# Output projection behind an RWKV scan: PSUM tiles, load queues, load order, and the engine of two group norms

## Chip, cores and metric

The kernel runs on one core of a Trainium2 chip. The metric is the device time of one execution in microseconds (us). TensorE is called PE (its weight loads PEld), VectorE DVE, ScalarE ACT, GpSimd POOL and SyncE SP, as in the profile. ACTq and SPq are DMA issues on the queues of ACT and SP.

## What is computed

One step of a two-layer diffusion trunk with model width 1024 over 640 tokens: 512 latent tokens and 128 prompt tokens. Layer 0 mixes tokens with a bidirectional RWKV-7 scan, layer 1 with neighbourhood attention, and each is followed by a squared-ReLU MLP. The change lies at the end of layer 0's mixer, which in the reference is this, with `ys` the outputs of the forward and the backward scan:

```python
y = (ys[0] + ys[1]).astype(jnp.float32)
mean = jnp.mean(y, axis=-1, keepdims=True)
var = jnp.mean(jnp.square(y - mean), axis=-1, keepdims=True)
yn = ((y - mean) * lax.rsqrt(var + GN_EPS)).reshape(B, T, D) * ln_w + ln_b
o = (yn + (bonuses[0] + bonuses[1]).reshape(B, T, D)) * g
return o.astype(h.dtype) @ w_o, jnp.stack(finals, axis=1)
...
x = x + gt1[:, None, :] * o
```

## The kernel before

**Layout and arithmetic.** The activations lie with the 1024 features on 8 blocks of 128 partitions and the 640 tokens along the free axis. A product of two f32 matrices is made from three fp32r products: each operand is split into a high part (a cast on ACT) and a low part (a subtraction), and PE adds high x high, high x low and low x high in PSUM. So a weights block of 1024 x 128 goes through a DMA of 512 KB, a cast on ACT and a subtraction on DVE before PE can use it.

**The scan and the group norms.** `phase_scan` runs the recurrence in five steps of four sub-steps, two directions at a time. PSUM is fully shared out here: two banks `A0`, `A1` for the products of the directions, two banks `B0`, `B1` for their running state (`self.G`), and two tiles `pp0`, `pp1` of two banks each. When both directions have passed a half of a 128-token tile, `post_half` (L1114) takes that half: it loads V, the bonus factors `bc` and the gates `gs` (SP, L1129 to L1131), subtracts the mean (L1139), squares (ACT, L1140), makes the inverse root in many small DVE steps (`rsqrt`, L252), does five more operations on 128 x 512 elements (L1146, L1147, L1149 to L1151), turns the result with four PE transposes into `pp1` (L1154), multiplies by the gates (DVE, L1160) and stores it to a DRAM scratch, `o_d` (SP, L1162). The argument `on_dve` says whether L1139 and the five are put on DVE or on POOL. The last two halves are (3,1), tile 3, and (0,0), tile 0: L844 gives (3,1) to POOL and (0,0) to DVE. The buffer `pbuf`, into which V and the gates are loaded, exists once for each of the two parities of half.

**The first part of the projection.** `wo_first` (L1182) multiplies by `w_o` those 384 tokens whose `o` is finished before the last halves: it runs beside the end of the scan. It goes over 8 output blocks, k0 to k7, each with 24 matmuls of 384 columns (L1219). `weights(k)` loads a block into one of the two `adaraw` buffers on SP (L1189), casts it (L1191) and subtracts (L1192) into one of two `ww` pairs. The products of k go into one half of the two-bank tile `pp0`. The residual input is loaded into one of three `wr` buffers by two DMAs on ACT's queue (L1215, L1216), 128 and 64 KB; DVE multiplies the product by the gate and adds it (L1221, two instructions), and SP stores the sum to a DRAM scratch `xa_d` (L1222). The load into a `wr` buffer has to wait for the store of k-3.

```python
if k % 2 == 0:
    pa = self.pp_tile(0)
ps = pa[:, 512 * (k % 2):512 * (k % 2) + NA]
hi, lo = W[k] if k < 2 else weights(k)
```

**The second part.** `phase_wo` (L1224) does the same for the other 256 tokens, whose `o` came from the last halves. Its buffers lie where the scan's lay. SP loads the residual input `xi` (two DMAs of 512 KB, L1237), then `ol`, the finished `o` (eight of 128 KB, L1242), then the first part's results `xa` (eight, L1251). Each of eight blocks k has 24 matmuls of 256 columns (L1265) into one of four `psl` banks; DVE adds the residual (L1269), which reads `xi`; ACT squares the new x for the next norm (L1271), and PE sums the squares over the features (L359). The MLP of layer 0 follows.

**What sets the order.** The kernel is written as one program, and the order of the instructions on each engine and queue is fixed when it is built (L1587, with a simulated timeline as its guide): an instruction may be taken ahead of an earlier one of its engine if it seems ready. On the chip each engine and queue then keeps that order. The scan's matmuls and, late in the scan, the transposes of `post_half` are chained to one another by hand (`mm`, L850); the matmuls of `wo_first` are not.

Of the kernel before, what the change touches and what calls it, by code (L numbers as in the profile page):

```python
# [8 lines left out]
F32 = mybir.dt.float32  # L9
# [7 lines left out]
P = 128  # L17
D = 1024
KT = 8
TS = 512  # L20
# [152 lines left out]
class K:  # L173
# [248 lines left out]
    def pool(self, st, name, bufs, **k):  # L422
        return st.enter_context(self.tc.tile_pool(name=name, bufs=bufs, reuse_waits="tile", **k))
# [349 lines left out]
    def phase_scan(self, st):  # L773
        nc, tc = self.nc, self.tc
        if True:
            pool = lambda name, bufs, **k: self.pool(st, name, bufs, **k)
            self.yp = pool("yp", 4)
            adp = pool("adp", 2)
            one = pool("one", 1)
            self.ch = pool("ch", 1, space=PSUM)  # L780
            self.post = pool("post", 2)
            self.G = [self.ch.tile([P, 512], F32, name=f"B{d}").rearrange("p (a b v) -> p a b v", a=2, b=4) for d in range(2)]
            self.lnwb = one.tile([P, 2, 256], F32, name="lnwb")
            nc.scalar.dma_start(self.lnwb, self.A["lnwb"].rearrange("p (a x) -> p a x", a=2))
            self.cst2 = st.enter_context(ExitStack())
            self.c_slots(self.pool(self.cst2, "c2", 1), 4, 1)
            for d in range(2):
                self.gu[d].append(one.tile([P, 2, 2, 4, 64], F32, name=f"GU{d}1"))
                for h in range(2):
                    nc.gpsimd.memset(self.gu[d][1][64 - 64 * h:96 - 64 * h, h], 0.0)  # L790
            self.gi = [0, 0]
            self.yt = {}
            self.ydone = {}
            todo, running = [], []
            ada = [(0, b) for b in range(8, 24)]

            def ada_next():
                if ada:
                    pa = self.pp_tile()
                    pa = pa[:, :256]  # L800
                    self.ada_sums.append(self.ada_first(*ada.pop(0), adp, pa, self.mm))

            self.ada_sums = []
            done = {(0, 3): [(4, 0), (4, 1)], (3, 1): [(2, 0), (1, 1)], (3, 3): [(2, 1), (1, 0)],
                    (4, 1): [(3, 0), (0, 1)], (4, 3): [(3, 1), (0, 0)]}
            pend = None
            self.pin = True
            for n, ts in enumerate(self.steps):
                for e in range(4):
                    s0, s1 = (self.chain_step(ts, n, e, d) for d in range(2))  # L810
                    next(s0)
                    if pend:
                        for x in pend:
                            next(x)
                        if n == 4 and not self.late:
                            self.late_pools()
                        for t in done.get((n, e - 1) if e else (n - 1, 3), []):
                            todo.append(self.post_half(*t, n == 4 and t[0] % 3))
                    f = (0, 1, 1, 2)
                    k = self.fill(f[0])  # L820
                    next(s0)
                    k += self.fill(f[1])
                    ada_next()
                    k += self.fill(f[2])
                    next(s1)
                    next(s0)
                    next(s0)
                    next(s1)
                    k = self.fill(f[3])
                    if k:  # L830
                        next(s1)
                    pend = [s1] if k else [s1, s1]
                    for x in running:
                        next(x)
                    m = 2 if n == 4 else 1
                    running, todo = todo[:m], todo[m:]
                    for _ in range(2):
                        for x in running:
                            next(x)
            for x in pend:  # L840
                next(x)
            for x in running:
                next(x)
            todo += [self.post_half(*t, i) for i, t in enumerate(done[4, 3])]  # L844
            for _ in range(3):
                for x in todo:
                    next(x)
            self.wo_first(adp)
# [333 lines left out]
    def wo_first(self, adp):  # L1182

        nc = self.nc
        NA = 384

        def weights(k):
            raw = adp.tile([P, 4, 256], F32, name="adaraw").rearrange("p a x -> p (a x)")
            nc.sync.dma_start(raw, self.A["w_o"][k].rearrange("p a x -> p (a x)"))  # L1189
            hi, lo = (self.wf[1].tile([P, D], F32R, name=f"ww{k % 2}{i}") for i in range(2))  # L1190
            nc.scalar.copy(hi, raw)  # L1191
            nc.vector.tensor_tensor(lo, raw, hi.bitcast(F32), op=ALU.subtract)  # L1192
            return hi, lo

        W = [weights(k) for k in range(2)]
        xs = []
        for f in range(8):
            if f % 2 == 0:
                ol = adp.tile([P, 4, 256], F32, name="adaraw").rearrange("p a x -> p (a x)")
            o = ol[:, NA * (f % 2):NA * (f % 2) + NA]  # L1200
            nc.sync.dma_start(o[:, :256], self.o_d[f, :, 128:384])
            nc.sync.dma_start(o[:, 256:], self.o_d[f, :, TS:])
            hi, lo = (self.wf[0].tile([P, NA], F32R, name=f"wx{f}{i}") for i in range(2))
            nc.scalar.copy(hi, o)
            nc.gpsimd.tensor_tensor(lo, o, hi.bitcast(F32), op=ALU.subtract)
            xs.append((hi, lo))
        gate = self.gate(0, 0)
        xv = self.A["xT"].rearrange("(k p) t -> p k t", p=P)
        for k in range(8):
            if k % 2 == 0:  # L1210
                pa = self.pp_tile(0)
            ps = pa[:, 512 * (k % 2):512 * (k % 2) + NA]
            hi, lo = W[k] if k < 2 else weights(k)
            xi = self.wf[min(k % 3, 1)].tile([P, NA], F32, name=f"wr{k % 3}")
            nc.scalar.dma_start(xi[:, :256], xv[:, k, 128:384])  # L1215
            nc.scalar.dma_start(xi[:, 256:], xv[:, k, TS:])  # L1216
            for f in range(8):
                for j, (a, b) in enumerate(((hi, xs[f][0]), (hi, xs[f][1]), (lo, xs[f][0]))):
                    nc.tensor.matmul(ps, lhsT=a[:, f * P:(f + 1) * P], rhs=b, start=(f == 0 and j == 0), stop=(f == 7 and j == 2))  # L1219
            for a, b, j in ((0, 256, 0), (256, NA, 1)):  # L1220
                nc.vector.scalar_tensor_tensor(xi[:, a:b], ps[:, a:b], gate[:, k, j:j + 1], xi[:, a:b], op0=ALU.mult, op1=ALU.add)  # L1221
            nc.sync.dma_start(self.xa_d[k], xi)  # L1222

    def phase_wo(self):  # L1224

        nc, tc = self.nc, self.tc
        with ExitStack() as st:
# [4 lines left out]
            xp = pool("xp", 8)  # L1232
            sp = pool("sp", 1)
            xv = self.A["xT"].rearrange("(k p) t -> p k t", p=P)
            xi = sp.tile([P, KT, 256], F32, name="xi")
            for o, t in ((0, 0), (P, 384)):
                nc.sync.dma_start(xi[:, :, o:o + P], xv[:, :, t:t + P])  # L1237
            ol = sp.tile([P, KT, 256], F32, name="ol")
            xs = []
            for f in range(0, 8, 2):  # L1240
                for o, t in ((0, 0), (P, 384)):
                    nc.sync.dma_start(ol[:, f:f + 2, o:o + P], self.o_d[f:f + 2, :, t:t + P].rearrange("f p t -> p f t"))  # L1242
            for f in range(8):
                xh = xp.tile([P, 256], F32R, name="xh")
                nc.scalar.copy(xh, ol[:, f])
                xl = xp.tile([P, 256], F32R, name="xl")
                nc.vector.tensor_tensor(xl, ol[:, f], xh.bitcast(F32), op=ALU.subtract)
                xs.append((xh, xl))
# [11 lines left out]
            for k in range(8):  # L1260
                w = self.wblock(self.A["w_o"][k])
                ps = self.psl.tile([P, 512], F32, name="psl")[:, :256]
# [4 lines left out]
                for i, r in enumerate((0, 1, 6, 7)):  # L1267
                    v = lambda a: a[:, 64 * i:64 * i + 64].rearrange("p (g j) -> p g j", g=8)
# [329 lines left out]
```

## Time and profile before

| | |
|---|---|
| median of 3 runs | 2234.46 us (2233.24 to 2239.57) |
| profiled execution, its own time | 2239.71 us |
| span from first to last instruction in it | 2237.9 us |
| mean granted TensorE clock in it | 0.944 |
| PE / DVE / ACT / POOL busy | 90% / 52% / 38% / 20% of the span |
| first part, k0 to k7 (L1219) | 765.3 to 832.7 us |
| second part (L1265) | 841.7 to 872.5 us |

All places are microseconds from the start of the span. "Busy" is the time in which an engine executes an instruction; waits for other engines are told apart from it, and each has a releaser: the instruction that ended last before the waiting one could start. The chain of waits follows these back from the last instruction. An engine that is idle costs nothing unless that chain goes through it. The granted clock is a share of the full 2.4 GHz; 0.5 is 1.2 GHz.

### The profile page before, as it was taken

How to read it: one execution, taken by the hardware profiler on the slowest of the kernel's cores; microseconds unless marked ns; L12 is line 12 of the kernel's file. 1: busy time of each engine (PE TensorE's matmuls, PEld its weight loads, DVE VectorE, ACT ScalarE, POOL GpSimd, SP SyncE). 2: the span in 40 equal slices, each digit the busy share in tenths (PEclk: the TensorE clock that was granted, in tenths of full speed). 3: DMA queues.
4: the chain of work that ended last, by engine and by line, in shares of the span. 5: the costliest groups of instructions: out<-in, count | busy, mean ns of one | idle time of the engine just before them, and what ended most of it. 6: DMA issues, size and time to landing. Idle time of an engine off the chain costs nothing.

```text
span 2237.9 us, 44938 instructions
## 1 busy us (share of the span) xinstructions
PE 2011.6 (90%) x18604; PEld 1827.3 (82%) x18604; DVE 1169.5 (52%) x2592; ACT 857.0 (38%) x1712; POOL 455.1 (20%) x553
## 2 busy tenths in 40 slices
PE   6999988757665569999999999999999999999999
PEld 3777777646554568999999998889677999999999
DVE  6656658387679755433333434433666633434342
ACT  4544553546553414313131323221576331313130
POOL 0001275656542411101010110000232110101010
PEclk8997999978787788999999999999899999999999
DMA  6455764545433464323232223343310232222221
GB/s 242 147 157 155 229 205 135 173 133 166 129 132 96 112 187 141 105 76 111 72 111 76 86 76 119 132 135 92 110 57 31 75 122 76 76 76 76 76 74 69
DMA packets 161037, 260.03 MB, mean 116 GB/s; under 512 B 46528, under 2 KB 102976, under 8 KB 160832
## 3 DMA queue, kind: packets, MB, share of 16 engines
q1 hardware_dynamic: 152224, 244.05, 35.2%
q10 hardware_dynamic: 8608, 13.11, 1.7%
q8 instruction: 146, 2.39, 0.4%
q14 instruction: 59, 0.48, 0.1%
HBM read 218.18 MB, written 37.35 MB: 114 GB/s over the span
## 4 chain that ended last, share of the span: by engine, by line
PE 74%; DVE 13%; DMA 5%; POOL 3%; issue 2%; ACT 2%; SPq 1%; DVEq 0%; ACTq 0%; POOLq 0%
PE psl L205 54%; PE psl L239 3%; DVE invX L996 2%; PE ps L1525 2%; DVE invT L993 2%; POOL C L947 2%; PE po L1562 2%; PE pp L852 2%; PE pt L1550 2%; DVE C L977 1%; PE pp L1219 1%; PE psl L1265 1%; PE psl L286 1%; DMA ld_s<-scr 1%; PE A L852 1%
## 5 line engine op out<-in xcount | busy, mean ns | idle before, releaser
L191 ACT CAST whi<-wraw 128x1024 fp32r<-128x1024 f32 x178 | 186.6, 1049 | 731.5 <-PE psl L205 701.9
L205 PE MATMUL psl<-xh,whi 128*128 128x320 f32 (+1 forms) x1696 | 414.6, 317 | 9.6 <-ACT xh L247 4.9
L205 PE MATMUL psl<-xl,whi 128*128 128x320 f32 (+1 forms) x1696 | 410.2, 314 | 1.2 <-DVE xl L248 1.2
L205 PE MATMUL psl<-xh,wlo 128*128 128x320 f32 (+1 forms) x1696 | 409.7, 314 | 0.4 <-DVE ta L592 0.4
L205 PEld LDWEIGHTS psl<-xh,whi 128*128 128x128 f32 x1696 | 291.4, 191 | 28.5 <-issue 8.7
L205 PEld LDWEIGHTS psl<-xl,whi 128*128 128x128 f32 x1696 | 292.5, 191 | 5.7 <-issue 3.2
L205 PEld LDWEIGHTS psl<-xh,wlo 128*128 128x128 f32 x1696 | 292.9, 191 | 2.6 <-issue 1.7
L1172 DVE SCALAR_TENSOR_TENSOR xres<-psl,mods,xres 128x320 f32<-128x320 f32 (+2 forms) x216 | 81.7, 434 | 305.1 <-PE psl L205 305.1
L1345 POOL TENSOR_TENSOR relu<-relu 128x640 f32<-128x640 f32 x64 | 80.2, 1255 | 773.9 <-ACT relu L1344 758.7
L205 PE MATMUL psl<-hhl,whi 128*128 128x320 f32 x1024 | 233.1, 308 | 0.0
L205 PE MATMUL psl<-hhh,wlo 128*128 128x320 f32 x1024 | 233.0, 308 | 0.0
L205 PE MATMUL psl<-hhh,whi 128*128 128x320 f32 x1024 | 232.9, 308 | 0.0
L193 DVE TENSOR_TENSOR wlo<-wraw,whi 128x1024 fp32r<-128x1024 f32 x178 | 218.6, 1229 | 11.6 <-ACT whi L191 10.9
L205 PEld LDWEIGHTS psl<-hhh,whi 128*128 128x128 f32 x1024 | 170.8, 188 | 0.4 <-issue 0.4
L205 PEld LDWEIGHTS psl<-hhh,wlo 128*128 128x128 f32 x1024 | 171.1, 188 | 0.0
L205 PEld LDWEIGHTS psl<-hhl,whi 128*128 128x128 f32 x1024 | 171.0, 188 | 0.0
L1302 DVE TENSOR_TENSOR relu<-psl,rms_b 128x320 f32<-128x320 f32 x128 | 60.8, 486 | 144.6 <-PE psl L205 144.0
L852 PE MATMUL pp<-C,KB 128*64 128x128 f32 x1280 | 100.6, 306 | 39.7 <-DVE C L977 16.7
L852 PEld LDWEIGHTS pp<-C,KB 128*64 128x64 f32 x1280 | 83.0, 154 | 54.1 <-issue 28.8
L248 DVE TENSOR_TENSOR hhl<-relu,hhh 128x640 fp32r<-128x640 f32 x64 | 53.4, 834 | 127.9 <-ACT hhh L247 127.7
L1052 ACT ACTIVATE GU<-A 32x256 f32<-32x256 f32 x160 | 60.0, 375 | 93.2 <-DVE mods L300 64.0
L977 DVE TENSOR_TENSOR C<-pp,cstsb 64x512 f32<-64x512 f32 x80 | 55.0, 688 | 69.1 <-ACT C L974 56.9
(299 smaller groups left out, 3393.2 us busy)
## 6 DMA issues: line engine op xcount, KB each, us to landing
wraw<-in_mlp_w SPq DMA_DIRECT2D x128, 512.0 KB, 3.5
adaraw<-in_ada_w SPq DMA_DIRECT2D x96, 512.0 KB, 4.9
ld_d<-scr SPq DMA_DIRECT2D x20, 512.0 KB, 4.5
ld_s<-scr SPq DMA_DIRECT2D x20, 512.0 KB, 3.7
bias<-in_bias SPq DMA_DIRECT2D x16, 384.0 KB, 3.7
scr<-ta SPq DMA_DIRECT2D x16, 325.0 KB, 3.5
wi<-scr SPq DMA_DIRECT2D x20, 260.0 KB, 4.6
scr<-bp SPq DMA_DIRECT2D x16, 320.0 KB, 4.5
```

The costliest lines, as they stand in the source:

```text
L191: nc.scalar.copy(hi, raw)
L193: nc.vector.tensor_tensor(lo, raw, hi.bitcast(F32), op=ALU.subtract)
L205: self.nc.tensor.matmul(ps[g][:, :e - c], lhsT=a[:, k, :], rhs=b[:, c:e], start=(k == 0 and j == 0), stop=(k == n - 1 and j == 2))
L239: nc.tensor.matmul(ps, lhsT=a[:, tc_], rhs=w, start=(k == 0 and j == 0), stop=(k == KT - 1 and j == 2))
L248: (lo_eng or nc.vector).tensor_tensor(xl, src, xh.bitcast(F32), op=ALU.subtract)
L852: r = (op or self.nc.tensor.matmul)(*a, **k)
L947: nc.gpsimd.tensor_tensor(rev(o) if s == 0 else o, v4(sh, s, ww)[hs], f[hs], op=ALU.mult)
L977: nc.vector.tensor_tensor(C[o, 8 * h:8 * h + 8, :], pn[o, :, 0:64], mask[o], op=ALU.mult)
L1052: nc.scalar.activation(gu[64 - 64 * hp:96 - 64 * hp, hp, pp].rearrange("p b v -> p (b v)"), U[32 * q:32 * q + 32, :], AF.Copy, scale=-0.5)
L1172: nc.vector.scalar_tensor_tensor(out[:, a:b], ps[g][:, o:o + b - a], gate[:, k, j:j + 1], x[:, a:b], op0=ALU.mult, op1=ALU.add)
L1302: nc.vector.tensor_tensor(t[:, c], ps[q][:, :HALF], rb[:, c], op=ALU.mult)
L1345: nc.gpsimd.tensor_tensor(t, t, t, op=ALU.mult)
```

## The change

Four edits. The first part puts k2 and k3 into the two state banks of the scan, k4 and k5 into `A0` and `A1`, and k0, k1, k6, k7 into `pp0` as before. Its residual loads go from ACT's queue to SP's. The last two halves, (3,1) and (0,0), both get `on_dve=True`. In the second part the loads of `ol` are issued ahead of those of `xi`.

```diff
-            todo += [self.post_half(*t, i) for i, t in enumerate(done[4, 3])]
+            todo += [self.post_half(*t, True) for t in done[4, 3]]
             for _ in range(3):
                 for x in todo:
                     next(x)
...
         for k in range(8):
-            if k % 2 == 0:
+            if k in (0, 6):
                 pa = self.pp_tile(0)
-            ps = pa[:, 512 * (k % 2):512 * (k % 2) + NA]
+            if k in (2, 3):
+                ps = self.G[k - 2].rearrange("p a b v -> p (a b v)")[:, :NA]
+            elif k in (4, 5):
+                ps = self.ch.tile([P, 512], F32, name=f"A{k - 4}")[:, :NA]
+            else:
+                ps = pa[:, 512 * (k % 2):512 * (k % 2) + NA]
             hi, lo = W[k] if k < 2 else weights(k)
             xi = self.wf[min(k % 3, 1)].tile([P, NA], F32, name=f"wr{k % 3}")
-            nc.scalar.dma_start(xi[:, :256], xv[:, k, 128:384])
-            nc.scalar.dma_start(xi[:, 256:], xv[:, k, TS:])
+            nc.sync.dma_start(xi[:, :256], xv[:, k, 128:384])
+            nc.sync.dma_start(xi[:, 256:], xv[:, k, TS:])
...
-            xi = sp.tile([P, KT, 256], F32, name="xi")
-            for o, t in ((0, 0), (P, 384)):
-                nc.sync.dma_start(xi[:, :, o:o + P], xv[:, :, t:t + P])
             ol = sp.tile([P, KT, 256], F32, name="ol")
             xs = []
             for f in range(0, 8, 2):
                 for o, t in ((0, 0), (P, 384)):
                     nc.sync.dma_start(ol[:, f:f + 2, o:o + P], self.o_d[f:f + 2, :, t:t + P].rearrange("f p t -> p f t"))
+            xi = sp.tile([P, KT, 256], F32, name="xi")
+            for o, t in ((0, 0), (P, 384)):
+                nc.sync.dma_start(xi[:, :, o:o + P], xv[:, :, t:t + P])
```

## Rows read from the trace of the kernel before

**Rows 1.** First line of the page.

```profile
span 2237.9 us, 44938 instructions
```

**Rows 2.** Busy by stretch: length, PE, PEld, DVE, ACT, POOL (instructions); PEclk, DMA, GB/s.

```profile
786.50:809.50 23.00, 13.26 (x72) 12.37 (x73) 21.32 (x49) 4.80 (x6) 6.57 (x5) 0.96 0.84 246
809.50:817.60 8.10, 7.84 (x32) 7.31 (x32) 3.78 (x8) 0.94 (x1) 0.00 (x0) 0.68 0.34 113
817.60:833.60 16.00, 13.22 (x72) 12.35 (x72) 5.35 (x12) 1.34 (x3) 0.00 (x0) 1.00 0.46 133
833.60:841.70 8.10, 0.40 (x2) 0.30 (x2) 0.00 (x1) 0.43 (x2) 0.00 (x0) 0.60 1.01 275
...
845.40:872.50 27.10, 27.10 (x240) 27.10 (x239) 19.65 (x55) 17.29 (x34) 5.77 (x15) 1.00 0.17 49
```

**Rows 3.** Timeline of PE, first part: start, length, what, [idle before it <- releaser].

```profile
788.50 4.44 PE L1219 MATMUL pp<-wx,ww 128*128 128x384 f32 x24 [2.03 <-DVE wr L1221]
794.49 4.41 PE L1219 MATMUL pp<-wx,ww 128*128 128x384 f32 x24 [1.55 <-DVE wr L1221]
799.83 4.41 PE L1219 MATMUL pp<-wx,ww 128*128 128x384 f32 x24 [0.93 <-DVE rsq_t L262]
809.52 5.91 PE L1219 MATMUL pp<-wx,ww 128*128 128x384 f32 x19 [5.29 <-DVE wr L1221]
...
817.66 4.40 PE L1219 MATMUL pp<-wx,ww 128*128 128x384 f32 x24 [0.17 <-DVE wr L1221]
...
828.33 4.41 PE L1219 MATMUL pp<-wx,ww 128*128 128x384 f32 x24 [0.93 <-DVE wr L1221]
```

**Rows 4.** Waits, 690 to 842: waiting <- releaser: us, times, longest.

```profile
PE pp L1219 <- DVE wr L1221: 10.9, 6, 5.3
...
ACT ww L1191 <- DMA wr<-in_xT: 9.9, 2, 5.6
...
ACT GU L1052 <- DMA wr<-in_xT: 1.8, 1, 1.8
```

**Rows 5.** Timeline of DVE, first part.

```profile
787.71 0.74 DVE L1221 SCALAR_TENSOR_TENSOR wr<-pp,mods,wr 128x256 f32<-128x256 f32 x2
...
797.69 0.17 DVE L263 SCALAR_TENSOR_TENSOR rsq_t<-rsq_t,yvar 128x8 f32<-128x8 f32 x1
...
806.00 1.12 DVE L263 SCALAR_TENSOR_TENSOR rsq_t<-rsq_t,yvar 128x8 f32<-128x8 f32 x1
...
811.03 0.68 DVE L1151 TENSOR_TENSOR Y<-Y,pbuf 128x512 f32<-128x512 f32 x1
```

**Rows 6.** Timeline of POOL, the norm of half (3,1).

```profile
800.29 1.72 POOL L1146 TENSOR_TENSOR pbuf<-pbuf,bc 128x512 f32<-128x512 f32 x1 [18.86 <-DMA pbuf<-scr]
```

**Rows 7.** Timeline of SP's queue, both parts.

```profile
798.50 0.34 SPq L1222 DMA_DIRECT2D scr<-wr  x1
798.93 0.38 SPq L1189 DMA_DIRECT2D adaraw<-in_w_o  x1
...
834.03 1.12 SPq L1237 DMA_DIRECT2D xi<-in_xT  x2
835.27 5.36 SPq L1242 DMA_DIRECT2D ol<-scr  x8
```

**Rows 8.** Chain of waits, 755 to 842: start, length, what.

```profile
763.97 1.97 DMA adaraw<-scr
...
798.80 1.05 ACT ww L1191
...
799.88 1.23 DVE ww L1192
...
836.43 4.74 DMA ol<-scr
```

**Rows 9.** DMA issues, 780 to 850: KB each, median us to landing.

```profile
adaraw<-in_w_o SPq DMA_DIRECT2D x4, 512.0 KB, 4.8
...
xi<-in_xT SPq DMA_DIRECT2D x2, 512.0 KB, 5.1
```

## The prediction

> **What bounds the kernel now.** The page comes first, for the span: 2237.9 us [rows 1]. Time can be won only where TensorE (PE) stands, so the stretches around the changed code come next. The first part of the projection (k0 to k7, L1219) takes from 786.5 to 833.6 us, the second part (L1265) starts at 841.7. In the first, VectorE (DVE) is busy for 21.32 of 23.0 us up to 809.5 and PE for only 13.26; from 833.6 to 841.7 PE does 0.40 us of work; from 845.4 to 872.5 it is full, 27.10 of 27.10 [rows 2]. So the stage has two holes, one inside the first part and one between the parts, and whatever moves the second part's start moves everything behind it: what follows waits for PE's last matmul there.
>
> The PE timeline says what ends the holes. Each block of 24 matmuls takes 4.40 us, and ahead of every one stands a wait for DVE L1221, the evacuation of the block before: 2.03, 1.55, 0.93, 5.29, 0.17, and twice 0.93 us for k1 to k7 (k6, not shown, is as k7; the 0.93 ahead of k3 is put down to a small DVE step that ran beside L1221) [rows 3]. That holds for odd k too, which write the other half of the same two-bank tile, so the whole tile is handed over, not a half. In the waits this is PE's 10.9 us behind L1221 [rows 4]. The long one, ahead of k4, is a DVE queue matter: PE was done with k3 at 804.2, and its L1221 stood behind the last group norm's small steps, which took 1.12 us each while GpSimd (POOL) worked from 800.29 on, and 0.17 us before it [rows 5, 6]. POOL had itself waited 18.86 us for its V load [rows 6].
>
> The hole between the parts is the SyncE (SP) queue: the two xi loads at 834.03, behind them from 835.27 on eight ol loads in 5.36 us [rows 7], and the first ol lands 4.74 us after the chain takes it up at 836.43 [rows 8].
>
> **The change, part by part.**
>
> **Six banks.** k2 to k5 get a bank each, and k6 finds pp0 long empty. k1 still shares a tile with k0 and k7 with k6, so their waits (2.03 and 0.93) stay. Those of k2 to k6 go: 1.55 + 0.93 + 5.29 + 0.17 + 0.93 = 8.9 us. Next in line is then the weights pair of each k: once k-2 has been multiplied, a cast of 1.05 us and a subtraction of 1.23 us [rows 8], 2.4 us with the handovers, beside the 4.40 us of k-1: hidden. Before that the raw block must land, 4.8 us after its issue [rows 9], and it is issued when the subtraction of k-2 has freed its buffer: 2.4 + 4.8 = 7.2 us after k-4 ended, against the 8.8 us that two blocks take. That is hidden with 1.6 us to spare. If this cover goes, k4 to k7 pay about 1 us each: +4.
>
> Without the 5.29 us hole the clock should hold as well. The granted clock is 0.68 from 809.5 to 817.6 and 1.00 after it [rows 2], and 19 matmuls of k4 took 5.91 us, 311 ns each, where 24 of k5 took 4.40, 183 ns [rows 3]: 19 x 0.128 = 2.4 us. Sum so far: 11.3 us.
>
> **Both norms on DVE.** Six operations of 0.68 us [rows 5] come to DVE's queue, +4.1 us, and the POOL work of that stretch goes, beside which five small steps took 1.1 us in place of 0.17 (806.00 is one of them): -4.6. DVE therefore ends its norms where it does now (the last, L1151, ran from 811.03 [rows 5]) or, with the work of late k behind them, some 3 us earlier: 808.5 to 811. This is where I give something back. Each norm ends in four PE transposes, and they stand at a fixed place in PE's order. PE, without the holes, has k4 done at 788.50 + 4 x 4.43 = 806.2 and k5 at 810.6. If the transposes stand ahead of k5, PE waits 2.3 to 4.8 us for the norms; behind k5, nearly nothing. I take 2.3, between the two and nearer to the first since the old place was inside k4 and at its end. The first part then wins 9.0 us; the ends are 4.0 (4.8 for the norms, 2.5 for late weights) and 13.3 (k1's hole closes too, and nothing waits).
>
> **Residual loads on SP.** Sixteen small issues leave ACT. There, ACT's own weight casts stood 9.9 us in all behind them [rows 4], since a load into a wr buffer has to wait for the store of k-3. That takes the casts off a blocked queue; I count no time for it, because the casts are hidden once PE runs through. On SP each issue is under half a microsecond, by its neighbours (0.34 us for a store, 0.38 for a weights load [rows 7]): 16 x 0.4 = 6.4 us of SP time over 47 us. It costs nothing as long as SP idles between issues; what is queued behind a waiting xi load is the next raw weights block and the store of the k in hand, and DVE and PE wait for the block. Two issues ahead of each block are 0.8 us, half of its 1.6 us of slack. Of its own the move is bounded by a gain of 1.8 us (the last scan steps' GU copies on ACT stood that long behind such a load [rows 4]) and a loss of 3.2 us (four blocks late by 0.8). I take zero, since both sides have slack.
>
> The Trainium skill (DMA: Bandwidth & Descriptors, section "Issuing engines are not separate DMA queues") holds that loads from any engine share the same DMA engines, so that another issuer saves only issue time. By it this part is worth nothing on ACT's side and loads SP. The trace adds what that rule leaves out, the 9.9 us of casts queued behind the issues; the sum is the same by both.
>
> **o first.** The two xi issues, 834.03 to 835.27, leave the head: 1.24 us. The first ol then also has no 1 MB ahead of it on the DMA engines. Its landing is bounded by 4.74 us (as now) and by 1.97 us (an o load of the first part on a quieter machine [rows 8]), a gain of 0 to 2.8. But the matmuls of k0 need all eight ol loads, whose issue takes 5.36 us whatever the order, so PE would reach the last pair sooner than it lands. I take 1.8 of the 2.8: 3.0 us in all, ends 1.2 and 4.0. xi now lands after the ol loads, about 5 us behind its issue [rows 9], which is about when k0 ends; its evacuation, L1269, may start late, but the four psl banks let PE run on for three more k.
>
> **The sum.** 9.0 + 3.0 = 12.0 us. The profiled execution took 2239.71 us, 5.25 above the median of 2234.46; the part outside the span is 1.8 us and unchanged. 2239.7 - 12.0 = 2227.7, or 2222.5 on the median's footing.
>
> **The rivals.**
>
> **A. DVE's queue is the new bound.** The V rows of the (3,1) half landed only at 800.29, where POOL waited for them [rows 6]. That wait now stands in DVE's own queue, with L1221 and the weights subtractions behind it. If L1146 is placed near 796, DVE stands for 4.5 us, the norms end near 814, and the first part wins 4.5: 7.5 in all, 2227. For: DVE has just 1.7 us free of 23.0 [rows 2]. Against: the squares on ACT come earlier, so other norm work is there to go first.
>
> **B. The banks free nothing.** Each engine's order is fixed when the kernel is built; if the weights of k4 to k7 keep their present times, PE merely waits for them instead. Only the second part's 3.0 remains: 2231.5. Against: k4's subtraction was over at 801.1 [rows 8], 8.4 us before k4 began.
>
> **C. SP holds back the weights: slower.** Now the weights of k5 are issued at 798.93, right behind the store of k1 [rows 7], four blocks ahead. With xi loads in the same queue, each waiting for a store to land, the weights of k could come to stand behind the store of k-1. Each block then costs evacuation 0.74, issue 0.3, landing 4.8, cast 1.05, subtraction 1.23 and handovers 0.4 [rows 5, 8, 9], or 8.5 us on top of 4.4. For k5 to k7, from 806.2, the end is 806.2 + 3 x 12.9 = 844.9 in place of 832.7: 12 us slower, less 3.0, that is 2243.5. It decides from the point where the weights of k are issued behind the store of k-2 (period about 8 us, level with now). Against: a raw block's buffer is free before that store is due, and a builder that fills idle queue slots takes it first. The sentence of the Trainium skill above leans to C's side.
>
> **How the numbers follow.** Forecast 0.55 (2217 to 2229), A 0.23, B 0.10, C 0.12. A measurement of this kernel can tell about 0.3%, 6.7 us, from no change, so faster means below 2227.8: the forecast nearly whole (0.54) and most of A (0.18), 0.72. Same: the rest of A, B and the forecast's edge, 0.16. Slower: C, 0.12. The range takes the sum's ends, 17.3 and 5.2 us of gain (2217.2 and 2229.3), with the runs' 1 us below, and reaches to B above: 2216 to 2232; C is left out.
>
> **What would show it.** Right: the waits for L1221 gone ahead of k2 to k6 and still there ahead of k1 and k7; k4's matmuls near 183 ns; no POOL operation of the norms after 780; the first L1265 matmul 4 to 5.5 us after the last L1222 in place of 8; PE's second part no longer than now. A shows as DVE idle ahead of L1146 with "DMA pbuf" as the releaser; B as PE waiting for L1192; C as raw weights landing after PE is done with k-1. The forecast is wrong if the first part still ends after 829, or if PE waits inside the second part for xi.

## The result, and the profile after

On one chip the changed kernel took 2224.2 us (median of 7 runs, 2223.14 to 2230.86), the kernel before 2239.57 us (7 runs, 2233.24 to 2247.47): ratio 0.9946, 95% interval 0.9929 to 0.9963, faster by more than the 0.3% that can be told from no change. The median that the forecast started from, 2234.46, was that of the first three of those seven runs. The profiled execution after took 2227.32 us.

The first line of the page after, for [rows 1], and its busy times by stretch (columns as in [rows 2]): the first part, the hole between the parts, the second part.

```profile
span 2225.5 us, 44926 instructions
```

```profile
791.85:827.00 35.15, 31.92 (x209) 30.22 (x208) 28.94 (x72) 7.87 (x10) 0.00 (x0) 1.00 0.82 243
827.00:831.30 4.30, 0.40 (x2) 0.30 (x2) 0.07 (x3) 0.44 (x2) 0.00 (x0) 0.94 0.86 275
831.30:867.00 35.70, 33.82 (x272) 33.44 (x272) 24.67 (x68) 21.58 (x44) 8.99 (x16) 0.93 0.43 134
```

PE is busy for 31.92 of 35.15 us at a granted clock of 1.00, and POOL does nothing there. Before, POOL had 6.57 us in the DVE-full stretch, and the clock fell to 0.68 behind it [rows 2]. The timeline of PE in the first part, for [rows 3] (L1224 is L1219 of before, L1226 is L1221, L1227 is L1222, L1244 is L1242, L1270 is L1265):

```profile
791.85 0.66 PE L852 MATMUL A<-GU,C 128*32 128x64 f32 x32
793.28 0.62 PE L1224 MATMUL B<-wx,ww 128*128 128x384 f32 x2 [0.78 <-ACT ww L1191]
794.63 4.43 PE L1224 MATMUL pp<-wx,ww 128*128 128x384 f32 x24 [0.72 <-DVE wr L1226]
798.89 8.14 PE L1224 MATMUL B<-wx,ww 128*128 128x384 f32 x46
806.87 4.68 PE L1224 MATMUL A<-wx,ww 128*128 128x384 f32 x26
812.17 4.09 PE L1224 MATMUL A<-wx,ww 128*128 128x384 f32 x22 [0.63 <-DVE ww L1192]
816.10 0.60 PE L852 MATMUL pp<-cstsb,Y 128*128 128x128 f32 x4
816.46 4.41 PE L1224 MATMUL pp<-wx,ww 128*128 128x384 f32 x24
820.99 0.63 PE L852 MATMUL pp<-cstsb,Y 128*128 128x128 f32 x4
821.79 4.41 PE L1224 MATMUL pp<-wx,ww 128*128 128x384 f32 x24 [0.17 <-DVE wr L1226]
```

The waits for an evacuation ahead of k2 to k6 are gone, and a new one of 0.63 us for a weights subtraction (L1192) stands ahead of k5. k1 and k7 start no sooner than before, measured from the work in front of them: k1 2.1 us after the scan's last product ends (2.0 before), with two matmuls of k2 (tile `B`, 793.28) in the gap and 0.78 and 0.72 us of idle time around them; k7 0.9 us after k6 (0.93 before), with the last transposes (820.99) in the gap and 0.17 us idle. The seven waits before came to 11.8 us, these four to 2.3; with the 2.4 us of slow clock that is 11.9 us. The queue of SP behind it, for [rows 7]:

```profile
822.44 0.37 SPq L1162 DMA_DIRECT2D scr<-pbuf  x1
823.11 0.89 SPq L284 DMA_DIRECT2D adaraw<-in_ada_w  x2
827.01 0.33 SPq L1227 DMA_DIRECT2D scr<-wr  x1
827.50 4.00 SPq L1244 DMA_DIRECT2D ol<-scr  x8
831.61 1.23 SPq L1247 DMA_DIRECT2D xi<-in_xT  x2
832.88 3.88 SPq L1256 DMA_DIRECT2D xa<-scr  x4
```

**A measure for all kernels.** One execution differs from the next by up to 16 us (the 30 runs of before beside the first experiments span 2227.07 to 2243.03), more than any single edit is worth. So I compare stretches inside the profiled executions, cut at five marks: the start of one B state product late in the scan, the same in each (721.21 before, 723.36 after), that of the scan's last A state product (785.82, 791.85), the last L1222/L1227 store of the first part (833.54, 827.01), the second part's first matmul (841.72, 831.32), and the end of its last sum over features (875.58, 866.96). "Rest" is what follows that. All in us:

| kernel | scan end | first part | hole | second part | rest |
|---|---|---|---|---|---|
| before | 64.6 | 47.7 | 8.2 | 33.9 | 1362.3 |
| after | 68.5 | 35.2 | 4.3 | 35.6 | 1358.5 |
| e1 | 64.9 | 36.5 | 4.4 | 35.0 | 1359.6 |
| e2 | 64.9 | 42.9 | 3.8 | 35.4 | 1363.2 |
| e3 | 65.4 | 40.8 | 4.3 | 35.3 | 1359.2 |
| e4 | 63.9 | 36.8 | 9.0 | 34.7 | 1363.8 |
| e5 | 64.6 | 38.8 | 3.9 | 35.5 | 1358.0 |
| e6 | 64.5 | 42.0 | 9.0 | 34.6 | 1357.9 |
| e7 | 67.4 | 42.1 | 8.5 | 34.6 | 1363.4 |
| e8 | 66.3 | 33.8 | 7.0 | 35.2 | 1357.8 |
| e9 | 67.6 | 35.1 | 10.1 | 33.6 | 1366.5 |
| e10 | 66.7 | 35.2 | 11.4 | 34.1 | 1362.2 |
| e11 (after again) | 65.1 | 36.5 | 4.5 | 36.1 | 1359.1 |
| e12 | 64.5 | 35.0 | 3.4 | 42.5 | 1359.4 |

Between before and after the first part gave 12.5 us, the hole 3.9, and the second part took 1.7 back: 14.7 us (e11: 11.2 + 3.7 - 2.2 = 12.7). The medians differ by 15.4, and by 12.5 in e11's set. No edit lies in the rest, which runs from 1357.8 to 1366.5. Its two groups go with the granted clock of one stretch of layer 1: from 660 to 640 us before the end it was 0.83 in the eight kernels whose rest is below 1360, and 0.55 to 0.74 in the other six. What precedes the first mark is not in the table and differs as much, from 711.3 us (e7) to 728.1 (e4).

The table holds one execution of each kernel, and before was traced once. The first part after, which e1, e4, e11 and e12 share but for a queue, took 35.0 to 36.8 us, so differences below 2 us say nothing. For some kernels the three stretches promise more than the runs give: 9.3, 13.8 and 9.1 us against before for e4, e8 and e10, where the ratios below stand for 2, 7 and -4 us. The traced executions of e8 and e10 were among their two fastest; what the others lost, and where, is not shown.

### The profile page after: what moved, and what is told of

Read it like the earlier page. It is cut to its first block, busy times and chain, and to the rows that moved or that the text cites. A ratio compares the mean times of both kernels' runs of the same rounds, so it can differ in the third digit from the quotient of the medians.

```text
span 2225.5 us, 44926 instructions
## 1 busy us (share of the span) xinstructions
PE 2014.0 (90%) x18604; PEld 1834.1 (82%) x18604; DVE 1164.5 (52%) x2598; ACT 856.4 (38%) x1712; POOL 450.7 (20%) x547
## 3 DMA queue, kind: packets, MB, share of 16 engines
q1 hardware_dynamic: 154528, 245.62, 35.3%
## 4 chain that ended last, share of the span: by engine, by line
PE 73%; DVE 13%; DMA 5%; POOL 3%; issue 3%; ACT 2%; SPq 1%; DVEq 0%; ACTq 0%; POOLq 0%
PE psl L205 55%; PE psl L239 3%; DVE invX L996 2%; DVE invT L993 2%; PE ps L1530 2%; PE po L1567 2%; POOL C L947 2%; PE pt L1555 2%; PE pp L852 1%; DVE C L977 1%; DMA wi<-scr 1%; PE psl L286 1%; PE st L565 1%; PE pk L698 1%; PE A L852 1%
## 5 line engine op out<-in xcount | busy, mean ns | idle before, releaser
L193 DVE TENSOR_TENSOR wlo<-wraw,whi 128x1024 fp32r<-128x1024 f32 x178 | 218.5, 1229 | 10.1 <-ACT whi L191 9.7
L852 PE MATMUL A<-GU,C 128*32 128x64 f32 x2560 | 59.0, 246 | 37.9 <-DVE Y L1067 18.3
```

Of the source, the lines that this page charges most:

```text
L852: r = (op or self.nc.tensor.matmul)(*a, **k)
```

## The experiments

**e1: residual loads back on ACT's queue.**

```diff
-            nc.sync.dma_start(xi[:, :256], xv[:, k, 128:384])
-            nc.sync.dma_start(xi[:, 256:], xv[:, k, TS:])
+            nc.scalar.dma_start(xi[:, :256], xv[:, k, 128:384])
+            nc.scalar.dma_start(xi[:, 256:], xv[:, k, TS:])
```

> The changed kernel with its residual loads back on ACT's queue. Marks: from the state product of the scan that begins at 721.21 us before and 723.36 after, to the scan's last state product, it is 64.6 us before and 68.5 after; from there to the last store of the first part 47.7 before and 35.2 after. Theory 1 (the four residual loads that the change puts into SP's queue at 742 us lengthen the scan's end): the first distance is 64 to 66 again, the second stays within 2 us of 35.2, and the kernel is 2 to 4 us faster than the changed one. Rival (ACT's casts, 9.9 us behind those loads before, were what held the first part): the second distance grows by 5 us or more and the kernel is slower than the changed one by 2 or more. Rival (the 3.9 us are scatter of one execution): the first distance stays near 68.5.

2226.3 us, ratio to before 0.9951 (0.9930 to 0.9971). The first part took 36.5 us, as in e11 with the loads on SP, so the queue changes nothing there. The scan's end took 64.9 us, which at first looked like a gain against the 68.5 of after; but the other kernels with loads on SP gave 63.9 to 67.6, among them the repetition of after (e11) 65.1. Those 68.5 us were one execution, and the gain of 2 to 4 us that the theory expected did not come. The Trainium skill (DMA: Bandwidth & Descriptors, section "Issuing engines are not separate DMA queues") says that another issuing engine saves only the issue time; this run agrees.

**e2: the old two-bank tile, with all other edits. e3: half (3,1) back on POOL, with all other edits.**

```diff
-            if k in (0, 6):
+            if k % 2 == 0:
...
-            if k in (2, 3):
...
+            ps = pa[:, 512 * (k % 2):512 * (k % 2) + NA]
```

```diff
-            todo += [self.post_half(*t, True) for t in done[4, 3]]
+            todo += [self.post_half(*t, i) for i, t in enumerate(done[4, 3])]
```

> The changed kernel with all eight products back in pp0. Theory (banks carry the first part's gain, 8.9 us of waits and 2.4 of clock): every block waits for the evacuation of the one before, the distance from the scan's last state product to the last store goes from 35.2 to 44 to 48 us, and the kernel is 9 to 12 us slower than the changed one, so about level with the one before. Rival (the norms on DVE and the freed ACT queue carry it): the distance stays under 40 and less than 5 us are lost. Rival (weights are the last wait anyway): the same, with PE waiting for the casts or subtractions.

> The changed kernel with half (3,1) on POOL again. Theory (no time by itself: six operations of 0.68 us more on DVE against five slowed steps, -4.6): the kernel is within 2 us of the changed one; the small DVE steps of 1.1 us beside POOL come back. Rival (DVE is now the bound, its subtraction for k5 ended PE's last hole of 0.63 us): with 4 us less on DVE the first part ends 2 to 4 us earlier. Rival (POOL slows DVE so that the weights come late): 3 to 6 us slower.

e2: 2233.68 us, 0.9986 (0.9969 to 1.0003); first part 42.9, between its theories. e3: 2233.03 us, 0.9978 (0.9959 to 0.9997); first part 40.8. Each edit is thus worth some 4 to 8 us with the other in place (k1 ran slow in e2, 24 matmuls in 6.00 us, as in e1, e4 and e11; against those e2 loses 6.1 to 6.4), and the norms' engine, which I had booked as a loss, is as large a part as the banks. Where e3 loses it: PE's timeline, ACT's cast of k5's weights, DVE's and POOL's timelines, and the busy times of the wait and of the matmuls behind it.

```profile
814.28 5.30 PE L1224 MATMUL A<-wx,ww 128*128 128x384 f32 x20 [3.45 <-DVE ww L1192]
```

```profile
808.57 1.05 ACT L1191 CAST ww<-adaraw 128x1024 fp32r<-128x1024 f32 x1 [4.62 <-DVE yrs L264]
```

```profile
808.78 0.97 DVE L259 TENSOR_SCALAR rsq_i<-rsq_i 128x8 int32<-128x8 int32 x1
...
809.99 1.15 DVE L263 SCALAR_TENSOR_TENSOR rsq_t<-rsq_t,yvar 128x8 f32<-128x8 f32 x1
...
811.37 1.12 DVE L262 TENSOR_TENSOR rsq_t<-rsq_i 128x8 f32<-128x8 f32 x1
...
813.00 1.22 DVE L1192 TENSOR_TENSOR ww<-adaraw,ww 128x1024 fp32r<-128x1024 f32 x1
```

```profile
808.68 1.04 POOL L1147 TENSOR_TENSOR Y<-Y,yrs 128x512 f32<-128x512 f32 x1 [0.90 <-DVE yrs L264]
809.81 1.30 POOL L1150 TENSOR_TENSOR Y<-Y,lnwb 128x512 f32<-128x512 f32 x1
811.19 1.27 POOL L1151 TENSOR_TENSOR Y<-Y,pbuf 128x512 f32<-128x512 f32 x1
```

```profile
810.80:814.28 3.48, 0.03 (x2) 0.00 (x1) 3.31 (x9) 0.59 (x1) 1.58 (x2) 1.00 0.20 56
814.28:819.50 5.22, 5.22 (x21) 5.19 (x22) 3.86 (x8) 0.00 (x0) 0.00 (x0) 0.67 0.58 176
```

Each long DVE step ends with the POOL operation that it ran beside: 809.75 with 809.72, 811.14 with 811.11, 812.49 with 812.46. k5's weights subtraction stands behind them in DVE's queue: its cast had ended at 809.62, and it starts at 813.00. PE waits 3.45 us for it, and then runs at a granted clock of 0.67: 20 matmuls in 5.30 us, 265 ns each, where 183 is the full pace. e3's second theory, that POOL slows DVE and the weights come late, fits; "no time by itself" falls.

**e4: the residual input ahead of o again, with all other edits.**

```diff
+            xi = sp.tile([P, KT, 256], F32, name="xi")
+            for o, t in ((0, 0), (P, 384)):
+                nc.sync.dma_start(xi[:, :, o:o + P], xv[:, :, t:t + P])
             ol = sp.tile([P, KT, 256], F32, name="ol")
```

> The changed kernel with xi loaded ahead of o again. Theory: from the last store of the first part to the first matmul of the second 8.2 us as before in place of 4.3, PE's second part itself 30.8 in place of 31.2, and the kernel 3 to 4 us slower than the changed one. Rival (the matmuls run into the late xi or xa loads, so that the order only moves the wait): less than 1 us slower.

2236.18 us, 0.9991 (0.9970 to 1.0012). The hole is 9.0 us against 3.8 to 4.5 with o first (after, e1, e2, e3, e5, e11); the second part is 34.7 against 35.0 to 36.1. The order is worth some 4.5 us in the hole, and about one of them is given back.

**e5: both last norms on POOL, all other edits in place.**

```diff
-            todo += [self.post_half(*t, True) for t in done[4, 3]]
+            todo += [self.post_half(*t, False) for t in done[4, 3]]
```

> The changed kernel with both last halves' norm operations on POOL. From the scan's last state product to the last store of the first part it is 35.2 us in the changed kernel (36.8 in the run with xi first, which has the same first part) and 40.8 with only (3,1) on POOL. Theory (what counts is that DVE's small steps are slowed beside POOL, and the weights subtractions stand behind them in DVE's order): twice the POOL work, more steps of about 1.1 us in place of 0.17, and 42 to 46 us. Rival (the amount of work on DVE counts): 8 us less of it than in the changed kernel, and 36 us or less.

2229.86 us, 0.9968 (0.9944 to 0.9991); first part 38.8, between what the two theories said, so both missed. PE's timeline at k5, and the same stretch by busy time:

```profile
813.09 3.56 PE L1224 MATMUL A<-wx,ww 128*128 128x384 f32 x19 [3.04 <-DVE ww L1192]
```

```profile
813.09:816.65 3.56, 3.56 (x21) 3.52 (x22) 2.23 (x4) 0.00 (x0) 3.30 (x3) 1.00 0.54 200
```

The same wait as in e3 is there, 3.04 us long; but here the clock held at 1.00 (187 ns a matmul), which is 1.6 of the 2 us between e3 and e5.

**e6: the kernel before with the new banks alone. e7: the kernel before with both norms on DVE alone.** Each is one hunk of the change, and nothing else.

```diff
 e6
-            if k % 2 == 0:
+            if k in (0, 6):
...
 e7
-            todo += [self.post_half(*t, i) for i, t in enumerate(done[4, 3])]
+            todo += [self.post_half(*t, True) for t in done[4, 3]]
```

> The kernel before with the six banks alone. Distance from the scan's last state product to the last store: 47.7 us before, 35.2 changed. Theory (banks and norms are two locks on one door: with the banks free, PE next waits for the weights of k5, whose subtraction DVE did at 809.9 to 811.1 behind the slowed steps): 40 to 43 us, PE idle ahead of k5 for 3 us or more with DVE L1192 as releaser. Rival (the banks carry 11.3 us by themselves, as the prediction summed): 36 to 37 us.

> The kernel before with both last norms on DVE, nothing else. Theory: the hole of 5.29 us ahead of k4 closes to about 1 us and the slow clock after it goes, but each block still waits for the one before: 42 to 45 us from the scan's last state product to the last store (42.9 with the residual loads on SP as well). Rival (the freed ACT queue made that gain): 46 us or more. Rival (the norms need the banks to be worth anything): 47 us.

e6: 2238.18 us, 0.9995 (0.9976 to 1.0015). e7: 2234.13 us, 1.0000 (0.9970 to 1.0030). No difference in time can be told for either, but the first part is 42.0 and 42.1 us: 5.7 and 5.6 less than before, and their sum, 11.3, is what both together give (10.9 to 12.5). Both lie where their theories put them. PE's and DVE's timelines of e6 at k5, then PE's of e7 for k2 to k5:

```profile
802.75 4.88 PE L1224 MATMUL A<-wx,ww 128*128 128x384 f32 x26
811.90 6.00 PE L1224 MATMUL A<-wx,ww 128*128 128x384 f32 x20 [4.27 <-DVE ww L1192]
```

```profile
808.98 1.13 DVE L262 TENSOR_TENSOR rsq_t<-rsq_i 128x8 f32<-128x8 f32 x1
...
810.63 1.22 DVE L1192 TENSOR_TENSOR ww<-adaraw,ww 128x1024 fp32r<-128x1024 f32 x1
```

```profile
787.51 4.40 PE L1219 MATMUL pp<-wx,ww 128*128 128x384 f32 x24 [1.60 <-ACT ww L1191]
792.84 4.41 PE L1219 MATMUL pp<-wx,ww 128*128 128x384 f32 x24 [0.93 <-DVE rsq_t L262]
798.00 0.66 PE L852 MATMUL pp<-cstsb,Y 128*128 128x128 f32 x4 [0.75 <-DVE Y L1151]
798.82 4.41 PE L1219 MATMUL pp<-wx,ww 128*128 128x384 f32 x24 [0.16 <-DVE rsq_t L263]
804.16 4.05 PE L1219 MATMUL pp<-wx,ww 128*128 128x384 f32 x22 [0.93 <-DVE wr L1221]
```

With the banks alone the 5.29 us hole ahead of k4 [rows 3] becomes a 4.27 us hole ahead of k5, again with slow matmuls behind it (300 ns each). In e6 too the cast was long done, at 806.72, and the subtraction began at 810.63. So the hole is not one of banks: it is DVE's queue, and PE meets it at the evacuation with the old banks and at the weights with the new ones. With the norms alone it is gone, and the 0.93 us per k of a shared tile stay.

**e8: banks in the order in which they come free, and half of the loads of o on ACT's queue.** k1 gets a state bank in place of pp0's second half, so its wait should go.

```diff
-            if k in (0, 6):
-                pa = self.pp_tile(0)
+            if k in (0, 5):
+                ps = self.pp_tile(0)[:, :NA]
...
-                    nc.sync.dma_start(ol[:, f:f + 2, o:o + P], ...
+                    (nc.sync if o == 0 else nc.scalar).dma_start(ol[:, f:f + 2, o:o + P], ...
```

> A version further: each product of the first part in a bank that its neighbours do not use (pp0, B0, B1, A0, A1, pp0, B0, B1), and the eight o loads of the second part issued half on SP, half on ACT. Theory: the waits ahead of k1 and k7 (0.72 and 0.17 us) go, 34 to 35.5 us for the first part; o is issued in 2 us in place of 4, and the first matmul of the second part comes 3 to 4 us after the last store in place of 4.3, with k0 done 1 us earlier relative to it. 1 to 3 us faster than the changed kernel in the trace, too little for the runs to tell. Rival (the DMA engines are the limit, 1 MB of xi now lies beside the second half of o): the hole stays at 4.3 or grows.

2230.51 us, 0.9967 (0.9943 to 0.9990). The first part is 33.8 us, the shortest; the hole is 7.0, not 3 to 4. The last half's o comes later than in the kernel after: the last step of its norm begins 30.6 us after the scan's last product (28.3 after), its transposes stand behind k7 in PE's order (818.11), the product with the gates (L1160) runs from 819.04, and its store is issued at 819.81, 34.5 us after that product (30.6 after). The loads of o wait for that to land, until 822.87. The sum of both stretches, 40.8, is no better than 39.5 (after) and 41.0 (e11): with PE faster, the path of the last half's o is the next bound.

**e9: the second part's first weights split later. e10: e8 with the same.** In the trace after, DVE spends 3.50 us at 790.42 on three subtractions that the second part needs 40 us later, ahead of k0's evacuation.

```diff
-                w = self.wblock(self.A["w_o"][k])
+                w = self.wblock(self.A["w_o"][k], (self.wo_last, self.o_last) if k < 3 else None)
...
+        for r, n in zip((c, v), after or ()):
+            self.tc.add_manual_dep(r.ins, n, ...
```

> The changed kernel with its second part's first three weight blocks split later: their subtractions, 3.50 us on DVE at 790.42 in the trace after, stand behind the last product with the gate, and their casts, 2.9 us on ACT at 789.36, behind the last cast of the first part's weights. Theory (the first part starts on a DVE that is nearly full, and these 3.5 us are on its path): k0's evacuation and the scan's last Y come 2 to 3.5 us earlier, the wait of 0.72 us ahead of k1 is gone, the first part takes 32 to 35 us where it took 35.2 to 36.8, the hole behind it stays at 3.5 to 5 because the three subtractions fit into it, the second part stays at 34.5 to 36; span 2 us below the control's at most. Rival (the 3.5 us lie beside PE's own 28 us of matmuls, and the parts end with PE): first part 35 to 37, nothing else moved.

> The kernel of e8_rotate_split (banks in the order in which they come free, half of the loads of o on ACT's queue) with the same later weight blocks. There the first part took 33.8 us but the hole behind it grew to 7.0, since the last half's norm, the multiplication with the gate and the store ended later than PE. Theory (that norm is the next bound, and it waits for DVE): with 3.5 us taken from DVE ahead of it, it ends 2 to 3.5 us earlier against the scan's last state product, the hole is 4 to 5 and from that product to the second part's first matmul it is 36 to 39 us (39.5 in the kernel after, 40.8 in e8). Rival (the norm's chain is bound by its loads and ACT's squares, not by DVE's queue): 40 to 42 as in e8.

e9: 2233.4 us, 0.9974 (0.9954 to 0.9995). e10: 2239.25 us, 1.0019 (0.9994 to 1.0043). Both miss. In e9 k1's wait did go, and the first part is 35.1, but the hole is 10.1 us. SP's queue in e9:

```profile
820.29 0.37 SPq L1166 DMA_DIRECT2D scr<-pbuf  x1
821.42 1.47 SPq L188 DMA_DIRECT2D wraw<-in_w_o  x2
822.99 0.38 SPq L287 DMA_DIRECT2D adaraw<-in_ada_w  x1
823.70 0.33 SPq L188 DMA_DIRECT2D wraw<-in_w_o  x1
824.12 0.39 SPq L287 DMA_DIRECT2D adaraw<-in_ada_w  x1
...
825.07 8.61 SPq L1249 DMA_DIRECT2D ol<-scr  x8
```

The raw weight buffers come free later, so three more 512 KB loads are issued just ahead of o; the eight loads of o take 8.61 us to issue in place of 4.00, and PE starts 9.6 us after the first of them. In e10 the same three loads stand at 825.28, between the last store of o (824.12) and the loads of o on SP (827.97). The last step of the last norm began 30.9 us after the scan's last product, against 30.6 in e8 (815.87 less 785.28): its chain did not get shorter with DVE emptier. DVE stood idle there for a square (1.75 us) and a load (0.75), as the rival had it, but also for a late weights cast and the products behind it (1.34 and 1.53), so the run does not decide.

**e11: the changed kernel once more.**

> The changed kernel itself, once more, as the measure of scatter for the two beside it and for the stretch of the scan. If its 68.5 us from the B state product to the last A state product were a cost of the residual loads on SP, they are 67 to 70 again; if they were scatter, 64 to 66.5. Either way the first part takes 35 to 37, the hole 3.8 to 4.5, the second part 35 to 36, and the ratio to the kernel before is 0.993 to 0.997.

2225.93 us, 0.9951 (0.9934 to 0.9968), beside e9 and e10. The scan's end took 65.1 us: scatter. Its first part is 1.3 us longer than after's because k1's matmuls ran slow there (24 in 5.99 us, as in e1), where after had 4.43.

**e12: the last store of the first part on ACT's queue.** After, the loads of o stand behind the store of k7 (827.01) in SP's queue, though the o that they load was stored at 822.44.

```diff
-            nc.sync.dma_start(self.xa_d[k], xi)
+            (nc.scalar if k == 7 else nc.sync).dma_start(self.xa_d[k], xi)
```

> The changed kernel with one store moved: the first part's last one, of k7, goes on ACT's queue instead of SP's. In the trace after it was issued at 827.01, once DVE had evacuated k7, and the eight loads of o stood behind it from 827.50 on, though the last half's o had been stored at 822.44. Theory (the hole between the parts now hangs on the order of SP's queue, not on the data): the loads of o start when that store of o has landed, about 3 us after its issue as in e8 (819.81 to 822.87), so at 825.5 to 826 on the scale of the trace after; from the last state product to the second part's first matmul it is 37 to 39 us (39.5 in the kernel after, 41.0 in its repetition), the hole 1.5 to 3, the second part 35 to 36.5. Rival (the first pair's landing is set by the 1 MB of other loads issued at 823.11, and comes no earlier): 39 to 41 and a hole of 3.8 to 4.5.

2226.4 us, 0.9937 (0.9918 to 0.9956), not to be told from after. From the last product to the second part it is 38.4 us, as the theory said; the hole itself is 3.4, between both theories. The profiled execution, the slowest of the six, then lost in the second part what it had won, and more. PE's timeline at its first wait there, and the busy times by stretch:

```profile
840.60 1.28 PE L359 MATMUL pq<-cstsb,sq 128*128 128x2 f32 x10 [0.88 <-ACT sq L1276]
```

```profile
840.00:842.00 2.00, 1.40 (x12) 1.40 (x13) 2.00 (x8) 2.00 (x5) 1.35 (x6) 1.00 0.79 205
842.00:845.00 3.00, 3.00 (x19) 3.00 (x19) 3.00 (x8) 3.00 (x7) 1.26 (x4) 0.61 0.78 267
...
848.00:852.00 4.00, 4.00 (x21) 4.00 (x20) 3.11 (x8) 2.76 (x5) 0.00 (x0) 0.50 0.01 4
...
856.00:860.00 4.00, 4.00 (x35) 4.00 (x34) 2.76 (x8) 2.00 (x5) 0.00 (x0) 0.96 0.00 0
```

PE waited 0.88 us for a square of the new x, which needs the first part's results, whose loads stand last in SP's queue; then it had 1.2 GHz (0.50) until 856, and the second part took 42.5 us. No version here is measurably faster than the change itself.

## Why the prediction was right

2222.5 us was forecast and 2224.2 measured, in the range of 2216 to 2232, and faster. The number is better than its working, and that is luck in two places. The gain was put at 12.0 us and is some 12.5 to 15.4, and the median that it was taken from lay 5 us below the one of seven runs: from 2239.57 the same sum gives 2227.6. And in the sum itself one term was twice too large and another had the wrong sign. By step:

**Six banks: 11.3 us forecast, 5.7 measured alone (e6).** The step that failed is the sentence that k2 to k6's waits go and that the weights are "hidden with 1.6 us to spare". The 1.6 us were worked out from landing, cast and subtraction; what is queued on DVE ahead of the subtraction was left out, although the same paragraphs had named that queue as the cause of the 5.29 us. e6 and e3 show PE waiting 4.27 and 3.45 us for L1192 there. Even with that queue cleared the slack was not there: after, PE waited 0.63 us, behind a raw block that came late.

**Both norms on DVE: -2.3 us forecast, +5.6 measured alone (e7), 4.0 to 5.6 with the banks (e3).** Twice wrong. The small steps slowed beside POOL (five of them, 0.96 to 1.15 us; the others kept 0.17) were counted as busy time of DVE and not as the PE hole and slow clock that hung on them. And the transposes that were to cost 2.3 us cost nothing: they stand behind k5 and k6 in PE's order (816.10, 820.99, no wait). The norms ended later than the 808.5 to 811 forecast, as DVE's timeline after shows:

```profile
790.42 3.50 DVE L193 TENSOR_TENSOR wlo<-wraw,whi 128x1024 fp32r<-128x1024 f32 x3 [0.73 <-ACT whi L191]
...
806.38 0.68 DVE L1146 TENSOR_TENSOR pbuf<-pbuf,bc 128x512 f32<-128x512 f32 x1
...
812.03 0.68 DVE L1151 TENSOR_TENSOR Y<-Y,pbuf 128x512 f32<-128x512 f32 x1
...
820.15 0.69 DVE L1151 TENSOR_TENSOR Y<-Y,pbuf 128x512 f32<-128x512 f32 x1
```

**Both together: 9.0 forecast, 10.9 to 12.5 measured** (47.7 less 35.2, 36.5, 36.5, 36.8 in after, e1, e11, e4). The waits that vanish were the right ones; two misattributions cancelled in their sum. k1's and k7's waits stayed, as forecast; PE only found other work to do in them.

**Residual loads on SP: 0 forecast, 0 measured** (36.5 in e1 and in e11). That both queues had slack, the reason given, is not shown by itself.

**o first: 3.0 us forecast.** Against e4 the hole shrank by 4.5 and the second part lost about 1: 3.5. Against before the two stretches give 1.5 (e11) to 2.2. The landing was worth 2.6 us, where 1.8 was taken: the first matmul came 6.45 us after the first load of o was issued before (835.27, 841.72) and 3.82 after (827.50, 831.32). That the second part would be "no longer than now" was wrong. xi held DVE's evacuation of k0 up by 0.75 us (838.91), which PE did not see; what PE met were the first part's results, the last loads in the queue. Before, their issue began 1.0 us ahead of the second part's first matmul (840.73, 841.72); after, 1.6 us behind it (832.88, 831.32). POOL's first copy of them, in the trace after, and PE's wait that hangs on it (PE waits 1.8 us for squares in all after, 0.8 before):

```profile
839.63 1.14 POOL L1258 COPY xres<-xa 128x256 f32<-128x256 f32 x1 [55.77 <-DMA xa<-scr]
```

```profile
842.12 1.28 PE L359 MATMUL pq<-cstsb,sq 128*128 128x2 f32 x10 [0.53 <-ACT sq L1276]
```

**The rivals.** A did not come: L1146 of half (3,1) ran at 806.38 with no idle time ahead of it, since other norm work was there to go first. B's mechanism, weights kept late by a fixed order, is what e6 and e3 show at k5, at about half of B's price; the norms edit is what removes it. C did not come, though the order that it feared is there: SP issued the weights of k5 at 804.72, right behind the store of k1 (804.05) and 3.5 us after their buffer had come free (k3's subtraction, 801.23), and those of k6 at 806.69, behind the store of k2. The residual loads are not its cause, for e6, with them on ACT, has the same order (801.53 behind the store at 800.80). The raw blocks held ACT's casts up. In the waits after:

```profile
ACT ww L1191 <- DMA adaraw<-in_w_o: 8.5, 3, 4.7
```

PE saw only 0.63 us of it, ahead of k5.

## What to carry to other kernels

A wait names the instruction that ended last, not the queue that made it late: before crediting an edit with removing a wait, ask whether what comes next for the waiting engine stands in the same queue. Two edits that each look worthless in the run times can be two halves of one gain; cut the traces at common marks to see it when executions scatter more than the edits are worth. Moving work on a full engine to a later time can move transfers into the one stretch where a load is on the path (e9).

## What was not expected of the hardware

**DVE steps of 0.17 us stretched to the end of a POOL operation** (e3: three steps of 0.97 to 1.15 us, each ending 0.03 us after POOL's). The Trainium skill (SBUF — State Buffer, section "Who interferes with whom") has DVE and GpSimd share a port pair as an exclusive lock; ends that coincide agree with that, and the price here is the whole remaining POOL operation for a step of 8 elements per partition.

**The clock after short holes.** After an idle time of 3.45 us with a granted clock of 1.00, PE got 0.67 (e3); after 3.04 us it kept 1.00 (e5). Ahead of k1, idle times of 1.30 and 0.72 us with two matmuls between them stood before 24 matmuls in 5.99 us (e1; a granted clock of 0.79 from 788 to 796), while 1.16 and 0.73 us stood before 24 in 4.43 (e3, full clock). In e12 it fell to 0.50 for some 13 us soon after a wait of 0.88 us, while PE was busy without a break; after and e11 had like waits, 0.53 and 0.79 us, and stayed at full clock behind them. What decides between these is not shown by any run here.
